# First mixers of a two-block transformer: products by c as ACT copies, forgetting heads without a query bias, division by the softmax sums at the end

## The chip, the core and the metric

The kernel runs on one core of one Trainium2 chip. The metric is the device time of one execution in microseconds (us). The engines of the core are TensorE (PE in the profile; PEld is its weight load), VectorE (DVE), ScalarE (ACT), GpSimd (POOL) and SyncE (SP, which issues most DMAs). They run side by side, each through its own list of instructions in order, and wait for each other by semaphores.

## What is computed

Two blocks over 512 tokens of width 1024, all in 32-bit floats. The first has a modulation from a vector c, four kinds of attention ("mixers") of four heads each, and a feed-forward part; the second has pooling, neighbourhood attention and sixteen experts. What the change touches:

```python
mod = c_act @ ada_w[l] + ada_b[l]          # c_act = silu(c); 1024 -> 6 x 1024
sh_a, sc_a, gt_a, sh_m, sc_m, gt_m = [m[:, None, :] for m in jnp.split(mod, 6, axis=-1)]
...
def forgetting_attention(q, k, v, f_logit, g_q, g_k):
    q = rmsnorm(q, g_q)
    k = rmsnorm(k, g_k)
    log_f = jax.nn.log_sigmoid(f_logit.astype(jnp.float32)).transpose(0, 2, 1)
    cum = jnp.cumsum(log_f, axis=-1)
    def block(i):                           # 128 queries
        s = jnp.einsum('bhqd,bhkd->bhqk', qb, k) * scale
        s = s + (cq[..., :, None] - cum[..., None, :])
        s = jnp.where(dist >= 0, s, NEG)
        p = jax.nn.softmax(s, axis=-1)
        return jnp.einsum('bhqk,bhkd->bhqd', p, v)
...
def neighbourhood_attention(q, k, v, q_norm, k_norm, rpb):   # second block
    s = jnp.einsum('bhcd,bhicjd->bhcij', q_r, k_nb) + bias
    pr = jax.nn.softmax(s.reshape(B, H, GRID_W, kh * WIN_COLS), axis=-1)
    return jnp.einsum('bhcij,bhicjd->bhcd', pr, v_nb)
```

## The kernel before

The program has four stretches. Up to about 60 us the input is normed. From there to about 460 us run the first block's mixers: eight units of two heads each, in the order s0, d0, n0, d1, n1, f0, f1, s1 (s is stick-breaking, d differential, n sparse, f forgetting attention). `run` keeps two units active, advances them step by step in turn, and feeds in between the projections that later units need (`diff_pre`, `fox_pre` and so on), then the output projection. From 460 to about 840 us comes the feed-forward part, to about 1016 us the second block's attention and pooling, and from there the experts, whose weights stream from memory. The order of instructions on each engine isn't written out: a scheduler places each instruction when its inputs are expected, by priority, so that any edit moves rows on every engine.

All mixers share one softmax: `softmax_part` (L610 to L618) adds a bias to the scores on DVE, takes the row's extreme, and lets ACT take the exponential and sum it into `l`. `scale_parts` (L636 to L642) then divides: a reciprocal, and one DVE multiply over each of the two heads' parts `e`. `transpose_p` turns `e` on PE (L626), DVE or ACT copy the result out as `pts`, and `pv` multiplies by the values (L648) into the tile `od`.

`fox` (L850 to L870) goes over four blocks of 128 queries with 128 to 512 keys. For each block and head it makes a bias tile `fb` on DVE: `ckb`, the running sum of the keys broadcast over the partitions, less the query's own `cqc` (L860), plus the causal mask over the last 128 columns (L861). `na` (L1183 to L1207) does four blocks for each of four pairs of heads in the second block.

`ada_more` (L347 to L366) forms four of the six modulation vectors on the side: 64 pieces of 128x512 weights, `adw`, in two buffers. Each piece is loaded by SP, multiplied on POOL by its column of c (L354), and added on POOL into `ada_a`, which has one buffer (L359; the first of eight pieces is copied instead, L357). After eight pieces PE sums over partitions (`pm`, L363). 48 pieces are strewn among the mixers' steps (`ada_side`, every third step), the rest among the first steps of the feed-forward part.

`rstd_rows` takes the sums of squares of a tile's rows and calls `rstd_of` (four small DVE and two small ACT instructions) on eight columns at a time. `to_features` spreads such a row statistic over a tile: one DVE copy `bc` (L392) and four PE transposes `rb` (L396).

## Time and profile before

| | us |
|---|---|
| median of 3 runs | 2147.28 (2143.96 to 2150.56) |
| the profiled execution | 2141.56 |
| its span, first to last instruction | 2139.8 |
| PE busy | 1930.0 |
| DVE busy | 851.3 |
| ACT busy | 555.9 |
| POOL busy | 242.7 |

The profiled execution is 5.7 us under the median, inside what single runs differ by (6.6 us between lowest and highest). All stretches below are given in us from the start of its span. Busy PE time is modelled, since matmuls overlap; the share of an engine is an average over stretches with different limits, so each stretch is read by itself.

### The profile page before, as it was taken

To read this page: it belongs to the slowest core of one execution; us is meant where nothing else is said; L and a number is where in the kernel's file an instruction comes from. 1 tells how busy PE (TensorE), PEld (TensorE's weight loads), DVE (VectorE), ACT (ScalarE), POOL (GpSimd) and SP (SyncE) were. 2 spreads that over 40 slices of the span, in tenths; PEclk is the share of its full clock that TensorE was granted. 3 is DMA by queue.
4 is the path that set the end of the run, shared out by engine and by line. 5 is a ranking of instruction groups with operands and counts; after the bars stand their busy time and mean duration, and the time that the engine had idled before them with its cause. 6 is when DMAs were issued, how large, how long until landed. Compare 5 with 4: busy or idle time off the path is not lost.

```text
span 2139.8 us, 22275 instructions
## 1 busy us (share of the span) xinstructions
PE 1930.0 (90%) x8534; PEld 1067.6 (50%) x8534; DVE 851.3 (40%) x1761; ACT 555.9 (26%) x1089; POOL 242.7 (11%) x211
## 2 busy tenths in 40 slices
PE   3898988979999998999899897878789999999997
PEld 2566666658888887776533232222233333333333
DVE  7887887874444335767431101210010111111114
ACT  4655545533333334444211001100000010000112
POOL 5530433350300000000000000000020000000001
PEclk9998999989999999999899899999989999999998
DMA  6532223243322222222889999799999999999992
GB/s 244 165 121 63 96 61 126 71 117 106 118 99 96 92 98 85 79 84 96 341 363 421 420 422 398 291 420 419 421 410 398 384 375 369 357 365 356 356 391 98
DMA packets 95082, 523.64 MB, mean 245 GB/s; under 512 B 11405, under 2 KB 12853, under 8 KB 44032
## 3 DMA queue, kind: packets, MB, share of 16 engines
q1 hardware_dynamic: 89936, 501.53, 60.6%
q0 software_dynamic: 3552, 17.82, 2.3%
q10 hardware_dynamic: 1488, 2.87, 0.4%
q8 instruction: 67, 1.10, 0.2%
q14 instruction: 39, 0.32, 0.0%
HBM read 510.83 MB, written 4.27 MB: 241 GB/s over the span
## 4 chain that ended last, share of the span: by engine, by line
PE 72%; DVE 11%; DMA 11%; ACT 3%; issue 3%; POOL 1%; POOLq 0%; ACTq 0%; DVEq 0%; SPq 0%
PE ua L1659 5%; PE ga L1659 5%; PE ga L1660 4%; DMA ch<-in_w_de_dram 4%; PE yd L1690 4%; PE ua L1660 4%; PE yd L1689 3%; PE pg L1594 3%; DMA ch<-in_w_ue_dram 3%; PE z L1609 3%; DMA xg<-xd,at 2%; PE od L648 2%; PE ag L331 2%; PE ag L332 2%; PE ag L333 2%
## 5 line engine op out<-in xcount | busy, mean ns | idle before, releaser
L1659 PE MATMUL ga<-ch,xe 128*64 128x512 f32 x512 | 244.4, 613 | 1.8 <-DMA ch<-in_w_ge_dram 1.8
L1660 PE MATMUL ua<-ch,xe 128*64 128x512 f32 x512 | 237.1, 611 | 5.9 <-DMA ch<-in_w_ue_dram 5.9
L1690 PE MATMUL yd<-ch,hts 128*64 128x512 f32 (+1 forms) x544 | 231.1, 572 | 10.4 <-DMA ch<-in_w_de_dram 10.4
L1659 PE MATMUL ua<-ch,xe 128*64 128x512 f32 x512 | 239.8, 612 | 0.1
L1660 PE MATMUL ga<-ch,xe 128*64 128x512 f32 x512 | 239.0, 610 | 0.5 <-DMA ch<-in_w_ge_dram 0.5
L1689 PE MATMUL yd<-ch,hts 128*64 128x512 f32 (+1 forms) x544 | 232.8, 572 | 0.0
L324 DVE TENSOR_TENSOR wlo<-pan,whi 128x1024 fp32r<-128x1024 f32 x119 | 154.6, 1299 | 157.0 <-ACT whi L321 153.9
L321 ACT ACTIVATE whi<-pan 128x1024 fp32r<-128x1024 f32 x119 | 125.9, 1058 | 211.7 <-PE ag L332 93.5
L1668 DVE TENSOR_TENSOR sg<-sg,ua 128x512 f32<-128x512 f32 x32 | 22.0, 687 | 340.2 <-PE ua L1660 340.2
L1690 PEld LDWEIGHTS yd<-ch,hts 128*64 128x64 f32 x544 | 70.1, 136 | 99.5 <-issue 76.5
L337 DVE TENSOR_TENSOR ys<-yg,ys 128x512 fp32r<-128x512 f32 (+1 forms) x17 | 12.5, 733 | 256.9 <-ACT ys L336 256.9
L1660 PEld LDWEIGHTS ua<-ch,xe 128*64 128x64 f32 x512 | 68.3, 140 | 83.0 <-issue 71.5
L1659 PEld LDWEIGHTS ua<-ch,xe 128*64 128x64 f32 x512 | 67.5, 140 | 80.7 <-issue 79.5
L1660 PEld LDWEIGHTS ga<-ch,xe 128*64 128x64 f32 x512 | 66.2, 139 | 74.4 <-issue 70.4
L1659 PEld LDWEIGHTS ga<-ch,xe 128*64 128x64 f32 x512 | 65.6, 139 | 70.8 <-issue 67.3
L1689 PEld LDWEIGHTS yd<-ch,hts 128*64 128x64 f32 x544 | 69.3, 136 | 56.4 <-issue 55.2
L1672 ACT ACTIVATE hts<-pth 128x512 f32<-128x512 f32 x32 | 19.1, 595 | 270.7 <-PE pth L1671 270.7
L1693 ACT ACTIVATE yg<-yd,gs 128x512 f32<-128x512 f32 (+1 forms) x17 | 11.3, 662 | 286.9 <-PE yd L1690 158.5
L354 POOL TENSOR_TENSOR adw<-adw,cT 128x512 f32<-128x512 f32 x64 | 77.4, 1210 | 41.3 <-DMA adw<-in_ada_dram 40.9
L359 POOL TENSOR_TENSOR ada_a<-ada_a,adw 128x512 f32<-128x512 f32 x56 | 78.0, 1393 | 4.4
L617 ACT ACTIVATE e<-e,m 128x256 f32<-128x256 f32 (+8 forms) x128 | 65.0, 509 | 51.2 <-DVE m L615 47.4
L1476 POOL DMA_INDIRECT xg<-xd,at x7 | 6.9, 979 | 594.8 <-DVE at L1474 590.4
(895 smaller groups left out, 3834.4 us busy)
## 6 DMA issues: line engine op xcount, KB each, us to landing
ch<-in_w_de_dram SPq DMA_DIRECT2D x128, 1024.0 KB, 13.6
ch<-in_w_ue_dram SPq DMA_DIRECT2D x125, 1024.0 KB, 8.9
ch<-in_w_ge_dram SPq DMA_DIRECT2D x120, 1024.0 KB, 12.4
pan<-in_w_up_dram SPq DMA_DIRECT2D x44, 512.0 KB, 3.2
adw<-in_ada_dram SPq DMA_DIRECT2D x64, 256.0 KB, 2.7
pan<-in_w_in_dram SPq DMA_DIRECT2D x24, 512.0 KB, 4.0
pan<-in_w_dn_dram SPq DMA_DIRECT2D x22, 512.0 KB, 3.3
adr<-in_adaT_dram SPq DMA_DIRECT2D x8, 1024.0 KB, 9.2
```

The lines of the kernel that those rows point to most:

```text
L321: A.activation(hi, raw, AF.Copy)
L324: eng.tensor_tensor(lo, raw, hi.bitcast(FT), op=OP.subtract)
L331: T.matmul(out, wh, xh, start=first, stop=False)
L354: P.tensor_tensor(w, w, cT[:, k:k + 1].to_broadcast([128, 512]), op=OP.mult)
L359: P.tensor_tensor(ada_next[1], ada_next[1], w, op=OP.add)
L617: A.activation(e[:, :nk], e[:, :nk], AF.Exp, bias=m, scale=-1.0, accum_out=l)
L1594: T.matmul(pg, xf[:, k], ple["wg"][k // 2][:, k % 2, S * h:S * h + S], start=k == 0, stop=k == 7)
L1609: T.matmul(zl[h], yts[at[k][0]][:, at[k][1]], ple["wg"][k // 2][:, k % 2, S * h:S * h + S], start=k == 0, stop=k == 7)
L1659: T.matmul(acc_[m][0:64], xe[:, kk, 0:64], wa[:, k], start=kk == 0, stop=kk == 7)
L1660: mm = T.matmul(acc_[m][64:128], xe[:, kk, 64:128], wb[:, k], start=kk == 0, stop=kk == 7)
L1689: T.matmul(yd[0:64], hts[:, kk, 0:64], wa[:, k_], start=kk == 0, stop=kk == 15)
L1690: mm = T.matmul(yd[64:128], hts[:, kk, 64:128], wb[:, k_], start=kk == 0, stop=kk == 15)
```

## The change

Four edits:

- In `ada_more` the product by a column of c is now the scale of an ACT copy. The first of eight pieces goes by it straight into `ada_a`, the others into `adw` in place; POOL only adds.
- In `fox` the query's own running sum is no longer subtracted: it is the same over a row, and the softmax doesn't see it. The causal mask is added in place to `ckb`, once for both heads, and the blocks run from the last to the first so that a masked stretch isn't read again. `cqc` and the copies that made it are gone.
- In `fox` and `na` the parts aren't divided any more. The sums of all four blocks stay in one tile, and the new function `divided` divides the output of a pair of heads once: a copy from PSUM, a reciprocal, `to_features`, one multiply. In `na` it goes through another tile, from which the two reordering copies read.
- `rstd_rows` calls `rstd_of` once for up to 16 columns; its two small tiles have 16 columns and four buffers.

```diff
-            P.tensor_tensor(w, w, cT[:, k:k + 1].to_broadcast([128, 512]), op=OP.mult)
             if k == 0:
                 ada_next[1] = tmp[0].tile([128, 512], FT, name="ada_a", tag="ada_a", bufs=1)
-                P.tensor_copy(ada_next[1], w)
+                A.activation(ada_next[1], w, AF.Copy, scale=cT[:, 0:1])
             else:
+                A.activation(w, w, AF.Copy, scale=cT[:, k:k + 1])
                 P.tensor_tensor(ada_next[1], ada_next[1], w, op=OP.add)
...
-        v, y = sm([128, 8], "rv")[0:n, 0:out.shape[-1]], sm([128, 8], "ry")[0:n, 0:out.shape[-1]]
+        v, y = [sm([128, 16], n_, 4)[0:n, 0:out.shape[-1]] for n_ in ("rv", "ry")]
...
-        for c in range(0, 4 * n, 8):
-            rstd_of(ms[:, c:min(c + 8, 4 * n)], scale, y[:, c:min(c + 8, 4 * n)])
+        rstd_of(ms[:, 0:4 * n], scale, y)
...
+    def divided(o, l, out):
+
+        A.activation(out, o, AF.Copy)
+        r = sm([128, 8], "r8", 2)
+        V.reciprocal(r, l)
+        V.tensor_tensor(out, out, to_features(r, 2), op=OP.mult)
...
     def fox(hp):
         q, kk, v, ckb = st["fox", hp]
         o = ps("od", "o", 2)
-        for i in range(4):
+        ls_ = sm([128, 4, 2], "l8", 2)
+
+
+        for i in (3, 2, 1, 0):
             nk = 128 * (i + 1)
-            l = sm([128, 2], "l2")
             e = []
+            V.tensor_tensor(ckb[:, :, nk - 128:nk], ckb[:, :, nk - 128:nk], K["cm"].unsqueeze(1).to_broadcast([128, 2, 128]),
+                            op=OP.add)
             for par in range(2):
-                h = 2 * hp + par
-                fb = t2k("fb")
-                V.tensor_scalar(fb[:, :nk], ckb[:, par, :nk], cqc[:, 4 * i + h:4 * i + h + 1], None, op0=OP.subtract)
-                V.tensor_tensor(fb[:, nk - 128:nk], fb[:, nk - 128:nk], K["cm"], op=OP.add)
                 s = ps("s", "s", 2)
                 scores(s, q, kk, par, slice(128 * i, 128 * i + 128), 0, nk)
-                e.append(softmax_part(s, fb[:, :nk], nk, l[:, par:par + 1]))
+                e.append(softmax_part(s, ckb[:, par, :nk], nk, ls_[:, i, par:par + 1]))
             yield
-            scale_parts(e, l, nk)
...
-        A.activation(mix[:, 2 + hp], o, AF.Copy)
+        divided(o, ls_.rearrange("p i h -> p (i h)"), mix[:, 2 + hp])
...
     def na(hp):
...
-            scale_parts(e, l, nk)
...
-        m, o = mix2[:, 4 + hp].rearrange("p (r c) -> p c r", r=8), o.rearrange("p (c r) -> p c r", r=8)
+        t = p2k("on")
+        divided(o, l.rearrange("p i h -> p (i h)"), t)
+        m, o = mix2[:, 4 + hp].rearrange("p (r c) -> p c r", r=8), t.rearrange("p (c r) -> p c r", r=8)
```

What the scheduler makes of it, first on DVE in forgetting attention. In the kernel before, around a block of 256 keys: `fb` is the bias tile, `e` a softmax part, `s` the scores, `m` the row's extreme, and the other rows belong to the sparse unit and to projections.

```order
L860 TENSOR_SCALAR fb<-ckb,cqc 128x256
L567 SCALAR_TENSOR_TENSOR sq<-pr,gsc,rb 128x512
L861 TENSOR_TENSOR fb<-fb,cst 128x128
L638 RECIPROCAL r_2922<-l_2882 128x2
L560 COPY pr<-acc__2989 128x512
L615 ISA e,m<-s,fb 128x256
```

And in the changed kernel, in the second forgetting unit from its second block on:

```order
L862 TENSOR_TENSOR ckb<-ckb,cst 128x2x128
L632 COPY pts<-pt 128x512
L614 ISA e,m<-s,ckb 128x384
L614 ISA m 128x1
L614 ISA e,m<-s,ckb 128x384
L614 ISA m 128x1
L862 TENSOR_TENSOR ckb<-ckb,cst 128x2x128
```

Of a block there remain on DVE one mask, two reductions with their small second row, and a copy of the transposed part; no row stands between the exponential on ACT and the transpose on PE.

Next on ACT, where the sparse unit's compressed keys begin (`kcv`). In the kernel before:

```order
L784 ACTIVATE kcv<-acc__954 64x512 x2
L321 ACTIVATE whi<-pan 128x1024
L617 ACTIVATE e,l_917<-e,m 128x128 x2
L574 ACTIVATE q_831<-sq 64x512 x2
L631 ACTIVATE pts<-pt 128x128
L617 ACTIVATE e,l_983<-e,m 128x256 x2
L321 ACTIVATE whi<-pan 128x1024
L617 ACTIVATE e,l_1011<-e,m 128x256 x2
```

And in the changed kernel:

```order
L787 ACTIVATE kcv<-acc__936 64x512 x2
L356 ACTIVATE ada_a<-adw,cT 128x512
L630 ACTIVATE pts<-pt 128x128
L616 ACTIVATE e,l_965<-e,m 128x256 x2
L358 ACTIVATE adw<-adw,cT 128x512 x2
L616 ACTIVATE e,l_993<-e,m 128x256 x2
L358 ACTIVATE adw<-adw,cT 128x512
L630 ACTIVATE pts<-pt 128x256
```

The products stand singly or in twos between the exponentials of the active units; each waits for its piece's DMA, and the one into `ada_a` for the `pm` of the eight pieces before it.

That `pm` stands on PE of the changed kernel just behind the projection that `kcv` is copied from:

```order
L654 MATMUL od<-pts,va 64x128
L703 MATMUL s<-k_724,k_480 128x256 x2
L333 MATMUL acc__936<-hTh,wlo 128x512
L363 MATMUL pm<-cst,ada_a 128x1 x4
L331 MATMUL acc__1223<-hTh,whi 128x512
```

In the kernel before POOL alone stood behind such a `pm`; now it is ACT, and behind ACT's product the exponentials.

On POOL a product and an addition stood in turn before; now additions alone stand there, 42 of them in one row.

## Rows read from the trace of the kernel before

**Rows 1.** The page: busy time by engine, and the chain by engine

```profile
PE 1930.0 (90%) x8534; PEld 1067.6 (50%) x8534; DVE 851.3 (40%) x1761; ACT 555.9 (26%) x1089; POOL 242.7 (11%) x211
...
PE 72%; DVE 11%; DMA 11%; ACT 3%; issue 3%; POOL 1%; POOLq 0%; ACTq 0%; DVEq 0%; SPq 0%
```

**Rows 2.** Stretches: length, busy PE, PEld, DVE, ACT, POOL, clock, DMA share, GB/s

```profile
60.00:460.00 400.00, 352.11 (x1874) 254.19 (x1872) 321.63 (x804) 202.67 (x489) 144.13 (x116) 0.94 0.32 99
460.00:840.00 380.00, 371.54 (x1631) 305.48 (x1630) 174.76 (x215) 131.81 (x161) 25.85 (x24) 0.99 0.30 101
840.00:1016.00 176.00, 171.76 (x875) 130.80 (x876) 120.83 (x318) 78.19 (x182) 6.82 (x13) 0.97 0.26 83
```

**Rows 3.** The chain: shares by line, 60 to 460; pieces as start, us, what

```profile
by line: PE od L648 6.8%; PE pt L626 5.8%; DVE e L642 3.8%; issue 3.6%; DVE wlo L324 3.2%; PE ms L382 3.0%; PE od L919 2.4%; PE s L816 2.4%; DVE e L615 2.2%; DVE e L705 1.8%; DVE q L575 1.6%; DVE sq L409 1.3%; DVE x L1013 1.3%; PE tl L914 1
...
277.88 2.37 DVE e L642 x2
```

**Rows 4.** Timeline (start, us) of DVE and of POOL at 66 us

```profile
66.65 3.36 DVE L324 TENSOR_TENSOR wlo<-pan,whi 128x1024 fp32r<-128x1024 f32 x1 [0.65 <-ACT whi L321]
...
66.87 2.04 POOL L354 TENSOR_TENSOR adw<-adw,cT 128x512 f32<-128x512 f32 x2
```

**Rows 5.** DVE groups, 60 to 460: count, busy us, mean ns, idle before

```profile
L324 DVE TENSOR_TENSOR wlo<-pan,whi 128x1024 fp32r<-128x1024 f32 x31 | 43.9, 1415 | 3.7 <-ACT whi L321 2.6 <-ACT ckb L846 0.7 <-PE acc__1241 L333 0.3
L642 DVE TENSOR_SCALAR e<-e,r 128x384 f32<-128x384 f32 x12 | 11.0, 954 | 0.1
L409 DVE TENSOR_TENSOR sq<-sq 128x512 f32<-128x512 f32 x7 | 10.4, 1480 | 2.2 <-ACT sq L407 2.2
L861 DVE TENSOR_TENSOR fb<-fb,cst 128x128 f32<-128x128 f32 x16 | 8.5, 532 | 0.3
L640 DVE TENSOR_TENSOR r<-r,gates 128x2 f32<-128x2 f32 x24 | 7.0, 291 | 0.4
L642 DVE TENSOR_SCALAR e<-e,r 128x128 f32<-128x128 f32 x12 | 6.5, 568 | 0.1
```

**Rows 6.** The same operations where POOL rests: 840 to 1016, and 480 to 840

```profile
L324 DVE TENSOR_TENSOR wlo<-pan,whi 128x1024 fp32r<-128x1024 f32 x20 | 24.4, 1221 | 0.4 <-ACT whi L321 0.2
L642 DVE TENSOR_SCALAR e<-e,r 128x248 f32<-128x248 f32 x24 | 7.3, 345 | 0.2
...
L409 DVE TENSOR_TENSOR sq<-sq 128x512 f32<-128x512 f32 x6 | 4.1, 684 | 0.0
```

**Rows 7.** POOL's two groups, 100 to 480

```profile
L359 POOL TENSOR_TENSOR ada_a<-ada_a,adw 128x512 f32<-128x512 f32 x42 | 58.5, 1392 | 3.3
L354 POOL TENSOR_TENSOR adw<-adw,cT 128x512 f32<-128x512 f32 x48 | 57.8, 1205 | 31.3 <-DMA adw<-in_ada_dram 31.0
```

**Rows 8.** Busy DVE time of lines L642, L860, L638, 60 to 460

```profile
60.00:460.00 400.00, 33.48 (x64) 0.94 0.32 99
...
60.00:460.00 400.00, 8.17 (x16) 0.94 0.32 99
...
60.00:460.00 400.00, 5.14 (x32) 0.94 0.32 99
```

**Rows 9.** Nearest rows to what is added: 60 to 460, 840 to 1016, page

```profile
L392 DVE COPY bc<-rs 128x512 f32<-128x512 f32 x13 | 6.6, 507 | 0.2
L567 DVE SCALAR_TENSOR_TENSOR sq<-pr,gsc,rb 128x512 f32<-128x512 f32 x6 | 4.5, 743 | 0.5 <-PE rb L396 0.5
...
L396 PE MATMUL rb<-cst,bc 128*128 128x128 f32 x32 | 5.8, 274 | 0.0
...
L1693 ACT ACTIVATE yg<-yd,gs 128x512 f32<-128x512 f32 (+1 forms) x17 | 11.3, 662 | 286.9 <-PE yd L1690 158.5
```

**Rows 10.** Waits, 100 to 480: us in total, times, longest

```profile
POOL ada_a L357 <- PE pm L363: 180.7, 5, 61.6
...
POOL adw L354 <- DMA adw<-in_ada_dram: 31.0, 24, 5.8
```

**Rows 11.** PE's weight loads of the transposes, 840 to 1016

```profile
L626 PEld LDWEIGHTS pt<-cst,e 128*128 128x128 f32 x40 | 5.5, 140 | 4.9 <-DVE e L642 2.1 <-DVE pts L633 0.6 <-DVE sq L567 0.6
```

More of the change, by code (lines that the diff above doesn't have):

```diff
@@ L722, in _build @@
     cum = pa.tile([4, S], FT, name="cum")
-    cqc = pa.tile([128, 16], FT, name="cqc")
     def gates_and_decay():
@@ L739, in gates_and_decay @@
         V.tensor_tensor_scan(cum, f2[0:4], f[0:4], 0.0, op0=OP.mult, op1=OP.add)
-        V.tensor_copy(t[0:4], cum)
         pg = ps("pg", "pt", 2)
@@ L746, in gates_and_decay @@
         V.tensor_scalar(gates[:, 0, 0:4], gates[:, 0, 0:4], K["vcol"], None, op0=OP.mult)
-        V.tensor_copy(cqc.rearrange("p (t c) -> p t c", t=4), pg[:, :, 0:4])
     def compress(kv):
@@ L1185, in na @@
         o = ps("od", "o", 2)
+        l = sm([128, 4, 2], "l8", 2)
         for b in range(4):
             nk = 248 if b else 256
-            l = sm([128, 2], "l2")
             e = []
@@ L1197, in na @@
                     T.matmul(s[:, :nk], q[:, par, 128 * b:128 * b + 128], k_, start=x_ == 0, stop=x_ == 1)
-                e.append(softmax_part(s, nb[:, par, 0:248] if b else nb[:, par, 248:], nk, l[:, par:par + 1]))
+                e.append(softmax_part(s, nb[:, par, 0:248] if b else nb[:, par, 248:], nk, l[:, b, par:par + 1]))
             yield
-            scale_parts(e, l, nk)
             pts = [transpose_p(e[par], nk, par) for par in range(2)]
```

## The prediction

> **What bounds the kernel now.** I read the page first, for the share of each engine in the chain that ended last [rows 1], and then the busy time by stretches, because such a share is a mean over stretches with different limits. In the stretch of the first block's mixers, 60 to 460 us, DVE is busy 321.6 of 400 us and PE 352.1; in the feed-forward stretch PE is busy 371.5 of 380, in the second block's attention 171.8 of 176 [rows 2]. The last two go by PE, and work taken off DVE there buys nothing by itself. The mixers go by nothing alone: there the chain changes between PE, DVE and a little ACT, and its largest DVE lines are the division of the softmax parts (L642, 3.8%) and the low parts of the weights (L324, 3.2%) [rows 3]. The third view is the same operation in and out of that stretch. `wlo` takes 1415 ns among the mixers and 1221 where POOL rests, the sum of squares L409 takes 1480 against 684 [rows 5, 6]. The timeline shows why: a `wlo` that starts at 66.65 lasts 3.36 us, and two products by c run on POOL from 66.87 for 2.04 us meanwhile [rows 4]. A DVE operation that meets a POOL operation stands until that one is over. So the mixers pay for POOL's work, though POOL itself is 1% of the chain [rows 1].
>
> **What the change does, part by part.** All sums are made against the profiled execution, 2141.56 us (a span of 2139.8 and 1.8 around it), and moved to the median of the runs, 2147.28, at the end; two executions differ by about 0.3% without a cause, and that is also what a measurement of this kernel can tell from no change.
>
> *Products by c leave POOL.* Five DVE groups tell what POOL costs DVE among the mixers. L324: 31 x (1415 - 1221) = 6.0 us. L642 on 384 columns: the row without POOL has 345 ns for 248 columns, so at most 534 for 384, and 12 x (954 - 534) = 5.0. L642 on 128 columns, at most 345: 12 x (568 - 345) = 2.7. L409: 7 x (1480 - 684) = 5.6. L640 against a reciprocal of the same two columns, 5.14 / 32 = 0.161: 24 x (291 - 161) = 3.1. Together 22.4 us [rows 5, 6, 8]. Groups that I leave out could double it. POOL's products have 57.8 us of the 116.3 that products and additions take [rows 7]; the additions stay. So half goes, 11.1 us. I count all of it on the path, because the stretched instructions are the ones that others wait for: a pair of L642, on 128 columns, stands in the chain with 2.37 us where two undisturbed ones would take at most 0.69 [rows 3, 6].
>
> *Forgetting heads.* The subtraction L860 goes: 8.2 us in 16 instructions [rows 8]. Of the masks L861, 8.5 us in 16 [rows 5], eight remain, twice as wide; they cost between half and all of that, and I take 3.0 saved. L642 has 64 instructions with 33.5 us among the mixers [rows 8], and 16 of them are the forgetting heads': 8.4. Eight reciprocals of 0.161 make 1.3. Sum 20.9 us.
>
> *Row statistics.* The four norms of the differential heads need one `rstd_of` each instead of two: 16 small DVE instructions of about 0.16, 2.6 us.
>
> *What comes back on DVE.* Two divisions of an output: a reciprocal 0.161, the copy `bc` 0.507, a multiply with one input in PSUM, whose nearest row is L567 with 0.743 [rows 9]. That is 1.4 each, 2.8 us.
>
> So beside the 11.1 us there are 20.9 + 2.6 - 2.8 = 20.7 us of DVE work less, 31.8 in all. How much of those 20.7 lies on the path? L642 has 3.8% of 400 us, 15.2, in the chain and 33.5 of busy time; L324 12.8 of 43.9; L409 5.2 of 10.4 [rows 3, 5, 8]. That is 33.2 of 87.8, some 0.4. I count 8.3 us, and DVE's part of the sum is 11.1 + 8.3 = 19.4.
>
> What one reads into these rows hangs on which engine is the limit. In the mixers DVE is busy 80% of the time and PE's weight loads 64% (254.2 of 400) [rows 2]. The Trainium skill, Perfetto Trace Analysis, section Identifying the Most-Contended Engine, says to judge DVE by its occupancy, PE by its weight loads rather than by its matmuls' busy time, and to count the engine that comes out highest as the one to relieve. By that rule DVE is the limit and the whole 31.8 us would come off, not 19.4. The chain disagrees so far: PE has 72% of it and DVE 11% over the kernel [rows 1].
>
> *Products on ACT.* An ACT copy with a column as scale: the nearest row is L1693, a Copy with such a scale, 662 ns [rows 9]. 48 of them among the mixers are 31.8 us, in a stretch where ACT is busy 202.7 of 400 [rows 2]. ACT has 3% of the span in the chain, 64 us of its 555.9 busy [rows 1]: 11.5%. So 3.7 us on the path; none if they fall into ACT's idle half, 31.8 if each delays an exponential that others wait for. The 16 in the feed-forward part lie under PE, which is busy there 98% of the time; without that cover they would cost 10.6.
>
> *New waits on ACT.* Each product waits for its piece's DMA. POOL stood 31.0 us for these, 24 times, because nothing else was queued there [rows 10]. On ACT the exponentials stand behind it. In ACT's order the products stand among other work, so that much of the landing has passed; I take half of the 31.0 and ACT's 11.5% of it, 1.8 us, between 0 and 31.0. The products that go into `ada_a` also wait for the `pm` of eight pieces before. POOL stood 180.7 us for that in 5 waits, up to 61.6 [rows 10]. On PE this `pm` stands directly behind the projection for which the ACT row ahead of the product waits too, so I put nothing for it; a place where PE is behind its order is part of the rival on ACT. SP's queue is involved as well: the next load of `adw` waits there for POOL's addition, and the weight panels are queued behind it. That was so before, with POOL's two operations in the loop instead of one of ACT and one of POOL.
>
> *PE.* Four transposes for each division, 0.274 us each [rows 9]: eight are 2.2 us among the mixers, of which PE's share of the chain, 72%, is 1.6.
>
> *The second block's attention.* 32 instructions of L642 and 16 reciprocals go, but PE is busy there 98%. What PE gets back is what it stood for them: 2.1 us at the weight loads of the transposes [rows 11]. It gets 16 transposes more, 4.4 us. Net 2.3 us slower. The last unit's output takes a copy and a multiply more before the reordering copies, some 1.4 us; the output projection's first half lies over it, and if that cover is short it costs up to this.
>
> Sum: -19.4 + 3.7 + 1.8 + 1.6 + 2.3 = -10.0 us. From 2141.56 that gives 2131.6, and from the median 2147.28 some **2137 us**. The prologue and the expert stretch have no edit and move as a whole with the start of their work.
>
> **Rivals.** *DVE is the limit of the mixers.* All 31.8 us come off and ACT's additions fall into its idle half: -31.8 + 1.6 + 2.3 = -27.9, so 2119; with the groups left out it could be 2108. For it speak DVE's 80% and the stretched pieces in the chain; against it PE's 88% of modelled busy time. This is what the skill's rule above amounts to.
>
> *PE is the limit of the mixers.* Then DVE's relief goes into waits that nobody notices, and PE's 2.2 and the second block's 2.3 remain: +4.5, 2152, no change that can be told. For it speaks PE's share of the chain; against it that PE's lines in the chain are short pieces, transposes and products with the values, that start when DVE or ACT is done.
>
> *The additions hit instead.* POOL still runs the additions, 42 of 1.39 us [rows 7]. If a DVE operation that no longer meets a product meets an addition, the 11.1 us stay: -10.0 + 11.1 = +1.1, 2148. Against it speaks that POOL's busy time halves; for it, that the pieces then follow each other faster.
>
> *ACT becomes the one that others wait for.* Its products and their waits are 31.8 + 31.0 = 62.8 us. If half of that lies on the path, 31.4, the sum is -19.4 + 31.4 + 1.6 + 2.3 = +15.9, and the time 2163. It turns slower at all from 25% on the path ((19.4 - 3.9) / 62.8) and slower by over 0.3%, 6.4 us, from 35%. ACT's present 11.5% speaks against it; for it, that an engine works its list in order and that each softmax goes through ACT, so that one late `adw` holds up both active units. The place is the rows with two products in a row between exponentials.
>
> **How the numbers follow.** The forecast has a chance of 0.46, DVE as the limit 0.24, PE as the limit 0.11, the additions 0.09, ACT 0.10. The forecast by itself reaches from 2130 to 2144: DVE's share of 0.4 may be 0.2 or 0.6 (4 us each way), ACT's may be double or nothing (5.5). Some 0.35 of its 0.46 lie below 2140.8, where faster by over 0.3% begins, and 0.11 above. So faster is 0.35 + 0.24 = 0.59, the same 0.11 + 0.11 + 0.09 = 0.31, slower 0.10. The range reaches on the fast side to the rival of DVE with a part of the groups left out, 2110, and on the slow side over PE as the limit to 2156, with some of a mild case of ACT; it leaves out the bad case of ACT and a gain beyond all of DVE's relief.
>
> **What would show it.** In the changed kernel's profile, the stretch from 60 us to the end of the mixers should be some 12 us shorter, its DVE time about 32 us less and its ACT time about 32 more. `wlo` among the mixers should come half way from 1415 to 1221 ns; if it stays, the additions hit instead. ACT's waits on the DMA of `adw` and on `pm` should sum to under 16 us; much over that, with exponentials late behind them, shows the rival on ACT. The second block's stretch should be 2 to 3 us longer. The forecast is wrong if the mixers' stretch shrinks by DVE's whole relief, or if it doesn't while DVE's time does.

## The result, and the profile after

The changed kernel takes 2115.55 us, the median of 4 runs (2114.46 to 2117.49). The kernel before, on the same chip, takes 2148.92 (2143.96 to 2152.56). The ratio is 0.985, with an interval of 0.983 to 0.987: 1.5% or 33 us faster. The forecast was 10 us; the direction was right, the time lies in the range, and the gain is three times the one worked out. The profiled execution took 2117.49 us, 24 less than the one before; the latter was one of the shorter runs of its kernel. The executions of the kernel before differ with the mean granted clock of TensorE: twelve of them on one chip, taken beside the runs below, go from 2138.59 us at 0.966 of full speed to 2153.93 at 0.957. The four of the changed kernel lie between 0.963 and 0.966, and the two profiled executions have 0.965 and 0.966. So some 24 us is the difference at a like clock, and the other 9 may go with the clock; whether the change raises it isn't shown.

The page of the changed kernel: its span, the busy time by engine with its share and count, and the chain by engine, to be read against [rows 1].

```profile
span 2115.7 us, 22322 instructions
...
PE 1927.1 (91%) x8558; PEld 1070.2 (51%) x8558; DVE 803.3 (38%) x1665; ACT 595.6 (28%) x1149; POOL 156.7 (7%) x139
...
PE 71%; DMA 11%; DVE 6%; ACT 3%; issue 2%; POOL 0%; POOLq 0%; ACTq 0%; DVEq 0%; SPq 0%
```

DVE lost 48 us of busy time and POOL 86, ACT gained 40; in the chain DVE's share fell from 11% to 6%. The page says what moved between engines, not where the gain is. For that I cut both spans at the same places of the work: the first matmul of the feed-forward part, the pause on PE ahead of the second block's first norm, the router's first matmul, and the end. In each row: the stretch and its length, then busy PE, PEld, DVE, ACT and POOL, the granted clock, DMA's share and GB/s. First the kernel before (the mixers ran up to 466.6 us; [rows 2] were cut at 460):

```profile
60.00:466.60 406.60, 354.10 (x1882) 255.72 (x1880) 324.84 (x811) 204.48 (x494) 147.36 (x118) 0.94 0.32 99
466.60:840.00 373.40, 369.55 (x1622) 303.94 (x1622) 171.55 (x209) 130.00 (x157) 22.62 (x21) 0.99 0.30 100
840.00:1015.80 175.80, 171.56 (x875) 130.68 (x875) 120.83 (x318) 78.19 (x182) 6.62 (x13) 0.97 0.26 82
1015.80:2139.80 1124.00, 1013.62 (x4096) 363.23 (x4095) 187.91 (x369) 115.32 (x215) 34.34 (x40) 0.96 0.91 370
```

and the kernel after:

```profile
60.00:438.40 378.40, 351.01 (x1889) 257.15 (x1887) 282.06 (x751) 237.81 (x543) 70.86 (x53) 0.95 0.34 107
438.40:811.60 373.20, 369.86 (x1622) 304.12 (x1622) 170.34 (x208) 134.10 (x163) 13.08 (x14) 0.99 0.30 100
811.60:988.00 176.40, 171.71 (x890) 132.05 (x890) 116.75 (x283) 80.57 (x186) 6.36 (x12) 0.97 0.25 79
988.00:2115.70 1127.70, 1013.40 (x4096) 362.99 (x4095) 188.03 (x370) 115.32 (x215) 34.59 (x40) 0.96 0.91 369
```

The mixers are 28.2 us shorter, the feed-forward part and the second block's attention keep their length (-0.2 and +0.6), and the expert stretch is 3.7 longer. That last one has no edit, and the same work took between 1120 and 1128 us in the executions of the versions below; it is scatter. So in this pair the whole gain lies in the mixers. PE does the same work there (354.10 against 351.01) in less time. DVE is 42.8 us less busy, ACT 33.3 more, POOL 76.5 less.

DVE's 42.8 can be divided by the duration of single instructions. These are DVE's groups among the mixers of the kernel after (60 to 438.4 us: count, busy us, mean ns, idle before), to be read against [rows 5] and [rows 6]:

```profile
L324 DVE TENSOR_TENSOR wlo<-pan,whi 128x1024 fp32r<-128x1024 f32 x31 | 39.5, 1275 | 6.5 <-ACT whi L321 5.8 <-PE acc__936 L333 0.3
...
L408 DVE TENSOR_TENSOR sq<-sq 128x512 f32<-128x512 f32 x7 | 7.6, 1088 | 2.1 <-ACT sq L406 2.1
...
L639 DVE TENSOR_TENSOR r<-r,gates 128x2 f32<-128x2 f32 x24 | 5.7, 239 | 0.4
...
L641 DVE TENSOR_SCALAR e<-e,r 128x384 f32<-128x384 f32 x8 | 4.1, 541 | 0.0
L862 DVE TENSOR_TENSOR ckb<-ckb,cst 128x256 f32<-128x256 f32 x8 | 3.4, 421 | 0.1
...
L641 DVE TENSOR_SCALAR e<-e,r 128x128 f32<-128x128 f32 x8 | 2.0, 284 | 0.1
```

`wlo` came from 1415 to 1275 ns, where 1221 is undisturbed: 72% of the way, not half. The sum of squares (L409 before, L408 now) came from 1480 to 1088, half of the way to 684. The divisions of 384 columns fell from 954 to 541 and those of 128 from 568 to 284; where POOL does none of this work (x_noadd, below) they take 417 and 280, so that is three quarters of the way and nearly all of it.

What is left of the disturbance shows at single instructions. Two places of the timeline of the kernel after, DVE and POOL (start, us, and in brackets the idle time before):

```profile
250.46 0.16 DVE L707 RECIPROCAL r<-l 128x2 f32<-128x2 f32 x1
250.58 0.17 DVE L375 TENSOR_TENSOR rv<-rv,ry 128x8 f32<-128x8 f32 x1
250.66 1.25 DVE L709 TENSOR_TENSOR c<-r,ls 128x1 f32<-128x1 f32 x1
...
250.58 1.32 POOL L359 TENSOR_TENSOR ada_a<-ada_a,adw 128x512 f32<-128x512 f32 x1 [18.34 <-ACT ada_a L356]
```

```profile
420.67 1.78 DVE L408 TENSOR_TENSOR sq<-sq 128x512 f32<-128x512 f32 x1
...
420.45 1.44 POOL L359 TENSOR_TENSOR ada_a<-ada_a,adw 128x512 f32<-128x512 f32 x1 [0.79 <-ACT adw L358]
```

A product of one column, 128x1, takes 1.25 us: it starts at 250.66 and ends at 251.91, and POOL's addition ends at 251.90. The sum of squares starts at 420.67, the addition ends at 421.89, and the sum of squares ends at 422.45, 0.56 later; undisturbed it takes 0.68 in all. In both places DVE stands for nearly all of the time until POOL is done. Nothing of that appears as a wait; it is counted as busy time of DVE.

So I summed it over the mixers for every kernel below: for each DVE instruction the time above the lower quartile of its line and shape in the same whole trace, where that is over 60 ns. I call the sum the **stretch**. It is worked out from the rows of single instructions, not a row itself. POOL's count leaves out three DMA issues.

```
mixers of one execution  length   DVE busy  stretch (instr.)  ACT busy  POOL busy (instr.)
before                   406.6    325       56.4 (76)         205       147 (115)
after                    378.4    282       21.1 (29)         238        71 (50)
p_ada                    382.8    287       18.7 (23)         238        71 (50)
p_bias                   401.8    318       55.9 (72)         206       150 (115)
p_divfox                 413.1    322       53.9 (76)         206       151 (115)
p_rstd                   406.8    321       51.5 (71)         204       155 (115)
u_ada                    397.1    306       46.7 (70)         203       152 (115)
u_na                     380.0    282       20.6 (30)         238        71 (50)
u_rstd                   376.8    273       14.4 (19)         238        73 (50)
x_act2                   388.4    279       19.2 (25)         265        71 (50)
x_noadd                  367.4    260        0.0 (0)          241         3 (1)
x_lock                   391.0    292       33.4 (68)         238       130 (148)
x_memset                 383.7    276       17.9 (32)         237       122 (246)
f_dve                    377.9    288        0.0 (0)          208         3 (1)
```

Where POOL does none of this work (x_noadd, f_dve) the sum is 0, so it holds little else than standing for POOL. Before, 56.4 of DVE's 325 us were standing: 23.7 of it beside products and the copies that begin a group, 32.6 beside additions (each instruction is put to the one of POOL that it overlaps longest). After, 21.1 is left. Of the 42.8 us that DVE lost, then, 35.3 is stretch and only 7.5 is work. The length of a single execution varies by some us (p_divfox's mixers are longer than before's, its median time isn't), so the experiments are judged by their medians and the table by its large steps.

### The profile page after: what moved, and what is told of

It is laid out like the page before. It is cut to its first block, busy times and chain, and to the rows that moved or that the text cites. A ratio compares the mean times of both kernels' runs of the same rounds, so it can differ in the third digit from the quotient of the medians.

```text
span 2115.7 us, 22322 instructions
## 1 busy us (share of the span) xinstructions
PE 1927.1 (91%) x8558; PEld 1070.2 (51%) x8558; DVE 803.3 (38%) x1665; ACT 595.6 (28%) x1149; POOL 156.7 (7%) x139
## 4 chain that ended last, share of the span: by engine, by line
PE 71%; DMA 11%; DVE 6%; ACT 3%; issue 2%; POOL 0%; POOLq 0%; ACTq 0%; DVEq 0%; SPq 0%
PE ua L1662 6%; PE ga L1662 5%; PE ga L1663 4%; DMA ch<-in_w_de_dram 4%; PE yd L1693 4%; PE ua L1663 4%; PE yd L1692 3%; DMA ch<-in_w_ue_dram 3%; PE pg L1597 3%; PE z L1612 3%; DMA xg<-xd,at 3%; PE od L654 2%; PE ag L331 2%; PE ag L332 2%; PE ag L333 2%
## 5 line engine op out<-in xcount | busy, mean ns | idle before, releaser
L324 DVE TENSOR_TENSOR wlo<-pan,whi 128x1024 fp32r<-128x1024 f32 x119 | 149.6, 1257 | 163.0 <-ACT whi L321 160.4
L331 PE MATMUL ag<-hTh,whi 128*128 128x512 f32 x176 | 70.8, 403 | 2.2 <-ACT hTh L428 2.2
L1670 ACT ACTIVATE sg<-ga 128x512 f32<-128x512 f32 x32 | 19.0, 595 | 185.5 <-PE ga L1663 172.9
```

What stands on the lines that cost most here:

```text
L324: eng.tensor_tensor(lo, raw, hi.bitcast(FT), op=OP.subtract)
L331: T.matmul(out, wh, xh, start=first, stop=False)
```

## The experiments

Two theories stood for the 33 us. **A, the lock:** the products left POOL, DVE stands less for POOL, and the standing lay on the path. **B, the softmax path:** the forgetting heads lost a subtraction, half of their masks and the divisions, which shortens the chain from scores to probabilities. A third reading, that the loop of the loads turns faster with one POOL instruction less in it, shares A's edit and had to be told from it. Each run stands beside runs of the kernel before on the same chip, and ratios are to these. "Over" or "under the kernel after" is a difference of medians from different rounds. The medians of the kernel before in these rounds lie between 2147.08 and 2149.64, so such a difference is good to about 3 us.

### Each part alone, on the kernel before

**p_ada**: only the products, as scales of ACT copies.

```
-            P.tensor_tensor(w, w, cT[:, k:k + 1].to_broadcast([128, 512]), op=OP.mult)
             if k == 0:
-                P.tensor_copy(ada_next[1], w)
+                A.activation(ada_next[1], w, AF.Copy, scale=cT[:, 0:1])
             else:
+                A.activation(w, w, AF.Copy, scale=cT[:, k:k + 1])
                 P.tensor_tensor(ada_next[1], ada_next[1], w, op=OP.add)
```

> The kernel before with the products by c as scales of ACT copies and nothing else. Theory A (the lock: the time that DVE stands for POOL falls by far more than half, and all of it lies on the path): 15 to 25 us faster than before, with DVE's busy time among the mixers some 30 us less. Theory B (the gain comes from the shorter softmax of the forgetting heads): 3 to 8 us faster, as the prediction's own sum for this part, -11.1 + 3.7 + 1.8 = -5.6.

Measured: 2118.97 us against 2147.64, ratio 0.987 (0.984 to 0.991), 28.7 us faster. The rows of its mixers, the stretch first and then two DVE groups:

```profile
60.00:442.80 382.80, 347.81 (x1877) 257.58 (x1875) 286.46 (x810) 237.30 (x551) 71.47 (x53) 0.94 0.34 105
...
L324 DVE TENSOR_TENSOR wlo<-pan,whi 128x1024 fp32r<-128x1024 f32 x31 | 39.2, 1264 | 5.0 <-ACT whi L321 3.6 <-PE pt L626 0.7 <-ACT ckb L846 0.5
...
L409 DVE TENSOR_TENSOR sq<-sq 128x512 f32<-128x512 f32 x7 | 8.5, 1221 | 2.1 <-ACT sq L407 2.1
```

DVE executes 810 instructions as before (811), and is busy 38.4 us less: all of it is duration. This one edit brings most of the gain, more than A's 15 to 25 us and far more than B's 3 to 8. A stands as the main cause.

**p_bias**: only the forgetting heads without a query bias, the masks put on the key bias in place, the blocks in reversed order.

```
-        for i in range(4):
+        for i in (3, 2, 1, 0):
...
+            V.tensor_tensor(ckb[:, :, nk - 128:nk], ckb[:, :, nk - 128:nk], K["cm"].unsqueeze(1).to_broadcast([128, 2, 128]),
+                            op=OP.add)
...
-                fb = t2k("fb")
-                V.tensor_scalar(fb[:, :nk], ckb[:, par, :nk], cqc[:, 4 * i + h:4 * i + h + 1], None, op0=OP.subtract)
-                V.tensor_tensor(fb[:, nk - 128:nk], fb[:, nk - 128:nk], K["cm"], op=OP.add)
...
-                e.append(softmax_part(s, fb[:, :nk], nk, l[:, par:par + 1]))
+                e.append(softmax_part(s, ckb[:, par, :nk], nk, l[:, par:par + 1]))
```

> The kernel before with the forgetting heads' query bias left out, the mask added once in place and the blocks from last to first, and nothing else. By the prediction's sum 11.2 us of DVE work less, 0.4 of it on the path: 4 us faster. Theory A: 3 to 6. Theory B: 8 to 14 us faster.

Measured: 2138.24 us, ratio 0.996 (0.994 to 0.998), 9.4 us faster. DVE is 7.6 us less busy, and the stretch stays (55.9). That gain lies in B's range and above A's.

**p_divfox**: only the division of the forgetting heads' output at the end.

```
+    def divided(o, l, out):
+
+        A.activation(out, o, AF.Copy)
+        r = sm([128, 8], "r8", 2)
+        V.reciprocal(r, l)
+        V.tensor_tensor(out, out, to_features(r, 2), op=OP.mult)
...
-            scale_parts(e, l, nk)
...
-        A.activation(mix[:, 2 + hp], o, AF.Copy)
+        divided(o, ls_.rearrange("p i h -> p (i h)"), mix[:, 2 + hp])
```

> The kernel before with the division at the end in the forgetting heads only. By the prediction's sum 9.7 us of DVE work less, 2.8 back, 0.4 of that on the path, and 1.6 us more on PE: 1 us faster. Theory A: 0 to 3 us faster. Theory B (no DVE row between the exponential and the transposes): 6 to 12 us faster.

Measured: 2145.4 us, ratio 0.999 (0.997 to 1.001), no change that can be told. DVE is 3 us less busy. B expected 14 to 26 us of these two edits; they bring 11.6 together, most of it by the first. As the main cause B falls; as a smaller one it keeps those 9.4 us.

**p_rstd**: only the row statistics of four norms in one call on up to 16 columns, not two on 8.

```
-        v, y = sm([128, 8], "rv")[0:n, 0:out.shape[-1]], sm([128, 8], "ry")[0:n, 0:out.shape[-1]]
+        v, y = [sm([128, 16], n_, 4)[0:n, 0:out.shape[-1]] for n_ in ("rv", "ry")]
...
-        for c in range(0, 4 * n, 8):
-            rstd_of(ms[:, c:min(c + 8, 4 * n)], scale, y[:, c:min(c + 8, 4 * n)])
+        rstd_of(ms[:, 0:4 * n], scale, y)
```

> The kernel before with one call for up to 16 columns of row statistics, and nothing else. Both theories: within 2 us of the kernel before; 2.6 us of small DVE work goes.

Measured: 2152.07 us, ratio 1.003 (1.001 to 1.005), 4.4 us slower, just outside of no change. Fewer DVE instructions don't pay here.

The four medians add up to -28.7 - 9.4 - 2.2 + 4.4 = -35.9 us, and all parts together gave -33.4. Nothing large is missing.

### Parts taken back out of the kernel after

**u_ada**: the products go back to POOL (p_ada's diff reversed).

> The changed kernel with the products by c back on POOL. Theory A: loses 15 to 25 us of the 33 and ends 8 to 18 us faster than the kernel before. Theory B: loses 3 to 8 and stays 25 to 30 us faster than the kernel before.

Measured: 2136.19 us, ratio 0.996 (0.994 to 0.998), 20.6 us over the kernel after. Its mixers, and `wlo`:

```profile
60.00:457.10 397.10, 351.60 (x1886) 258.28 (x1884) 306.14 (x750) 202.38 (x486) 152.06 (x118) 0.94 0.33 102
...
L324 DVE TENSOR_TENSOR wlo<-pan,whi 128x1024 fp32r<-128x1024 f32 x31 | 44.3, 1430 | 1.5 <-ACT whi L321 1.3
```

With about the same number of DVE instructions (750 and 751) the stretch is back from 21.1 to 46.7 and `wlo` at 1430. That is A from the other side, inside its 15 to 25 us.

**u_na**: the neighbourhood heads' division back in each block.

```
-        l = sm([128, 4, 2], "l8", 2)
         for b in range(4):
+            l = sm([128, 2], "l2")
...
+            scale_parts(e, l, nk)
...
-        t = p2k("on")
-        divided(o, l.rearrange("p i h -> p (i h)"), t)
-        m, o = mix2[:, 4 + hp].rearrange("p (r c) -> p c r", r=8), t.rearrange("p (c r) -> p c r", r=8)
+        m, o = mix2[:, 4 + hp].rearrange("p (r c) -> p c r", r=8), o.rearrange("p (c r) -> p c r", r=8)
```

> The changed kernel with the neighbourhood attention's division back at each block. The prediction put that edit at 2.3 us slower, so this would be 2 us faster than the changed kernel; the trace of the changed kernel shows the second block's stretch as long as before, so 0 to 1 us of difference either way is expected, some 33 us under the kernel before.

Measured: 2115.2 us, ratio 0.985 (0.982 to 0.989), the same as the kernel after. In the second block the division costs and saves nothing that can be told.

**u_rstd**: the row statistics back in two calls (p_rstd's diff reversed).

> The changed kernel with row statistics in two calls of eight columns again. Alone that edit made the kernel before 0.3% slower, with nothing in its own work that could (it only takes instructions away). If that is the order of the whole list: within 4 us of the changed kernel, either way. If one call of 16 columns is itself worse (the first eight columns wait for the others): 4 to 8 us faster than the changed kernel.

Measured: 2111.92 us (2110.47 to 2114.56), ratio 0.984 (0.981 to 0.986). The interval overlaps that of the kernel after, but both directions of this edit, 4.4 and 3.6 us, say that the single call is no gain. This run also has less stretch than the kernel after (14.4 against 21.1), so its 3.6 us need not come from the call itself. Of the versions that compute the whole result it is the fastest measured.

### The suspected costs by themselves

**x_act2**: on the kernel after, a second ACT copy of each piece.

```
             k = m % 8
+            A.activation(w, w, AF.Copy)
             if k == 0:
```

> The changed kernel with a second ACT copy of each modulation piece ahead of the first: 48 copies more among the mixers, some 32 us of ACT. If ACT's added time lies on the path by its 11.5% of the chain: 4 us slower than the changed kernel. If each delays an exponential that others wait for: up to 32 us slower. If ACT's idle time takes it all: no difference.

Measured: 2120.8 us, ratio 0.986 (0.982 to 0.990), 5 us over the kernel after, with overlapping intervals. Its mixers, and ACT's waits for the loads (total, times, longest):

```profile
60.00:448.40 388.40, 358.47 (x1889) 264.56 (x1887) 279.02 (x751) 264.78 (x599) 71.42 (x53) 0.91 0.33 104
...
ACT adw L354 <- DMA adw<-in_ada_dram: 6.5, 9, 1.7
```

27 us more of ACT cost at most about 5 of time. They need not be ACT's: with the same 1889 matmuls PE is 7.5 us busier here than in the kernel after, at a granted clock of 0.91 against 0.95. The copies are cheap, as they would be if ACT's idle time took most of them; whether they are free isn't shown.

**x_noadd**: on the kernel after, no additions; each sum of eight pieces is replaced by its last piece, so the modulation is computed from an eighth of its terms.

```
                 A.activation(w, w, AF.Copy, scale=cT[:, k:k + 1])
-                P.tensor_tensor(ada_next[1], ada_next[1], w, op=OP.add)
             if k == 7:
+                ada_next[1] = w
```

> The changed kernel without POOL's additions (each sum is formed from its last piece alone, so the modulation is not the reference's); loads and ACT copies stay. It measures what POOL still costs. The changed kernel's trace shows DVE operations among the mixers some 20 us longer than where POOL rests. Theory A: 12 to 20 us faster than the changed kernel. If the additions' lock lies beside the path: 0 to 5 us.

Measured: 2101.1 us, ratio 0.978 (0.974 to 0.981), 14.5 us under the kernel after. Its mixers, and two DVE groups:

```profile
60.00:427.40 367.40, 351.20 (x1889) 261.66 (x1887) 259.13 (x751) 239.99 (x545) 3.36 (x4) 0.94 0.35 111
...
L324 DVE TENSOR_TENSOR wlo<-pan,whi 128x1024 fp32r<-128x1024 f32 x31 | 37.9, 1221 | 3.7 <-ACT whi L321 3.0
...
L408 DVE TENSOR_TENSOR sq<-sq 128x512 f32<-128x512 f32 x7 | 4.8, 689 | 2.3 <-ACT sq L406 2.1
```

With POOL silent both groups run at their undisturbed 1221 and 689 ns, and no instruction is stretched any more. What the additions still cost the kernel after is at most these 14.5 us.

**x_lock**: on the kernel after, two POOL products of 128x192 on a tile of their own behind each addition. They read and write, and nothing uses what they make; the next addition stands behind them on POOL, in this run and in the next alike.

```
-                P.tensor_tensor(ada_next[1], ada_next[1], w, op=OP.add)
+                done_ = P.tensor_tensor(ada_next[1], ada_next[1], w, op=OP.add)
+                with tc.issue_after(done_.ins):
+                    for _ in range(2):
+                        P.tensor_tensor(lk, lk, one.to_broadcast([128, 192]), op=OP.mult)
```

> The changed kernel with two more POOL multiplies of 128x192 behind each addition, in a tile of their own: POOL reads and writes on-chip memory about as long as with the products, but no load and no ACT copy waits for them. If what counted in the products was that DVE stands while POOL reads: 12 to 24 us slower than the changed kernel, and DVE operations among the mixers longer by 45 us or more in sum, as in the kernel before (56) against 21 in the changed one. If it was the loop of loads behind POOL on SP's queue: within 4 us of the changed kernel.

Measured: 2127.85 us (2125.55 to 2132.21) against 2147.08, ratio 0.992 (0.989 to 0.995), 12.3 us over the kernel after. POOL's new group and DVE's `wlo` among its mixers:

```profile
L364 POOL TENSOR_TENSOR lk<-lk,one 128x192 f32<-128x192 f32 x98 | 61.3, 626 | 3.8
...
L324 DVE TENSOR_TENSOR wlo<-pan,whi 128x1024 fp32r<-128x1024 f32 x31 | 41.3, 1331 | 6.4 <-ACT whi L321 5.6 <-PE acc__944 L333 0.3
```

**x_memset**: the same with four POOL memsets of that tile, which write and don't read.

```
+                    for _ in range(4):
+                        P.memset(lk, 1.0)
```

> The same with four memsets of 128x192 in place of the two multiplies: POOL is as busy, but only writes. In the trace before, a DVE operation beside a memset of 1.80 us kept its 0.69 us. If POOL's reads are what DVE stands for: within 4 us of the changed kernel. If any POOL work does it: as slow as with the multiplies.

Measured, on the same chip: 2117.27 us (2114.82 to 2119.71), ratio 0.987 (0.984 to 0.990), 1.7 us over the kernel after and not to be told from it. The same two groups:

```profile
L364 POOL MEMSET lk<- 128x192 f32 x196 | 52.4, 267 | 8.5
...
L324 DVE TENSOR_TENSOR wlo<-pan,whi 128x1024 fp32r<-128x1024 f32 x31 | 39.3, 1268 | 4.7 <-ACT whi L321 4.2
```

POOL was made 59 us busier by the one and 51 by the other. The reading products lengthened DVE's stretch by 12.3 us (21.1 to 33.4) and the kernel by 12.3; the memsets did neither that can be told (17.9, and 1.7 us). Between these two runs, which share a chip and nearly a clock in the mixers (0.92 and 0.93), lie 15.5 us of stretch and 10.6 us of time. So it is POOL's reads that cost, and not its time or its place in the loop of the loads. I had expected the stretch of x_lock to come back to 45 or more. It didn't: the new products last 626 ns, half of the old ones' 1205, and beside them a DVE instruction is stretched by 0.29 us in the mean, where it was 0.65 beside the old ones. The Trainium skill, SBUF — State Buffer, section Who interferes with whom, says that DVE and GpSimd share a port pair, which is an exclusive lock, and that a DVE instruction with two inputs in SBUF contends with a GpSimd instruction that reads SBUF, not with one that only writes. Both runs agree with it: of DVE's `TENSOR_TENSOR` instructions that ran beside the new POOL instructions and no others of POOL's, 22 of 33 were stretched in x_lock and none of 31 in x_memset. The memsets aren't wholly without effect: eight copies and products by a column lasted 61 to 152 ns longer beside them, 0.85 us in all.

**f_dve**: on the kernel after, product and addition as one DVE instruction; POOL does none of it, and ACT keeps only the first piece of each eight.

```
-                A.activation(w, w, AF.Copy, scale=cT[:, k:k + 1])
-                P.tensor_tensor(ada_next[1], ada_next[1], w, op=OP.add)
+                V.scalar_tensor_tensor(ada_next[1], w, cT[:, k:k + 1], ada_next[1], op0=OP.mult, op1=OP.add)
```

> The changed kernel with product and addition in one DVE instruction (weights times the column of c, plus the sum so far), 42 among the mixers at about 0.75 us, so 32 us of DVE more; POOL does nothing there and ACT's 42 copies go. DVE operations stand for nobody, 21 us less. If DVE's busy time decides: 32 - 21 = 11 us more of it, 5 to 9 us slower than the changed kernel. If ACT's copies and their waits cost more than 5 us: no difference or faster.

Measured: 2115.17 us, ratio 0.985 (0.982 to 0.988), the same as the kernel after. Its mixers, and two DVE groups:

```profile
60.00:437.90 377.90, 351.78 (x1892) 262.12 (x1890) 288.00 (x799) 208.32 (x493) 3.36 (x4) 0.94 0.34 107
...
L324 DVE TENSOR_TENSOR wlo<-pan,whi 128x1024 fp32r<-128x1024 f32 x31 | 37.8, 1220 | 3.5 <-ACT whi L321 3.4
L358 DVE SCALAR_TENSOR_TENSOR ada_a<-adw,cT,ada_a 128x512 f32<-128x512 f32 x49 | 36.6, 746 | 2.1 <-DMA adw<-in_ada_dram 1.1 <-ACT ada_a L356 0.9
```

DVE does product and addition of 49 pieces for 36.6 us and saves the 21.1 of stretch, and ACT saves 30. The 5 to 9 us that DVE's busy time was to cost didn't come. POOL's help with the additions is worth nothing in the kernel after. With the products on POOL too its help costs: u_ada is 21 us slower than this run.

## Why the prediction came out too small

**The step that failed is the term "Products by c leave POOL".** It was put at 11.1 us off, and with ACT's 3.7 and 1.8 the products' move was to bring 5.6. Alone it brought 28.7 (p_ada), with 37.7 us of stretch gone where the term has 11.1 (56.4 to 18.7), and 20.6 came back with it (u_ada). The mechanism was the right one; the size was made of two factors, the first far too small and the second somewhat.

- *The whole.* I took five groups' 22.4 us for all of what POOL cost DVE. The stretch over all groups was 56.4. I wrote that the groups left out could double it, gave that to a rival's lower end, and left the sum as it was. By the same summing over the trace of before, L642 alone had 13.8 over all its shapes, where I counted 7.7; left out were the differential heads' division L705 (3.9), L861 (3.9), `k` L582 (3.5), `kp` L906 (3.0) and others with less.
- *The half that stays.* I halved it by POOL's time. 35.3 of 56.4 went, 63%, and 67% in p_ada; between u_ada and the kernel after it is 55%. The additions alone stretch DVE by 21.1 after, where it was 32.6 beside additions before. In u_ada, with the products back, it is 21.1 beside additions too, so the products ahead of them don't explain it; why the additions hit less than before isn't shown by a run.

The third factor, "all of it on the path", was a little high. u_ada: 25.6 us more stretch for 20.6 us of time, and up to 25.6 if the 5 us of x_act2 are ACT's and are given back. x_lock: 12.3 for 12.3 against the kernel after, 15.5 for 10.6 against x_memset. x_noadd: 21.1 for 14.5. A microsecond of standing costs 0.7 to 1 us here.

The sentence that a DVE operation that meets a POOL operation stands until that one is over was too wide. Beside POOL's products, additions and copies in the trace of before, 45 of 68 `TENSOR_TENSOR` and 20 of 34 `TENSOR_SCALAR` instructions of DVE were stretched, but only 8 of 31 `SCALAR_TENSOR_TENSOR`, and none of the 32 reductions of the softmax (L615) and the 17 reciprocals.

**Forgetting heads and divisions: two errors that partly cancel.** For p_bias and p_divfox I counted 20.9 - 2.8 = 18.1 us of DVE work less, 0.4 of it on the path, and 1.6 of PE against it: 5.6 us. The busy time that p_bias and p_divfox took off is 7.6 + 3.0, because the old durations held stretch that I had counted already in the first term, and because neighbouring small DVE instructions overlap in the trace (in the rows above L375 ends at 250.75 and L709 has begun at 250.66). Yet the two gained 11.6 us: about all of what they took off counts. The 0.4 out of the chain's shares was too low and the work too high, and the two errors left half of the gain.

**Row statistics: wrong sign.** 2.6 us less work was expected; alone the edit costs 4.4, just clear of the noise, and 3.6 in the changed kernel, which isn't clear of it. One call has to wait for all of its columns' sums, where the first of two calls could start early; this is argued, no run shows it.

**ACT: right in size, as far as it is shown.** A copy took 716 ns where 662 was taken, 57 of them in all (50 in the row below). ACT's waits were 14.7 us for the loads and 3.9 for `pm`, for which the sum had nothing: 18.6 together, a little over the 16 that I had put as the sign. Here are those rows of the kernel after, ACT's group and its waits (total, times, longest):

```profile
L358 ACT ACTIVATE adw<-adw,cT 128x512 f32<-128x512 f32 x50 | 35.3, 716 | 15.0 <-DMA adw<-in_ada_dram 14.7
...
ACT adw L358 <- DMA adw<-in_ada_dram: 14.7, 16, 2.5
ACT ada_a L356 <- PE pm L363: 3.9, 2, 2.9
```

By x_act2 such a load costs at most about 5 us of time, against 5.5 in the sum. The rival on ACT is refuted.

**PE and the second block: small.** PE stayed at 351 us among the mixers (354 before). The second block was to be 2.3 us longer and is 0.6 longer, within scatter; u_na says the same, so that term isn't seen.

**The rivals.** "The additions hit instead" is refuted by the stretch, 56.4 to 21.1, and by `wlo` at 1275. "PE is the limit" is refuted by the mixers' 28 us at an unchanged PE. "DVE is the limit", 2119 with a lower end of 2108, came nearest. That the time lies in the range is owed to this rival, for whose sake the range reached so far, and not to the forecast. By its own condition DVE's whole relief comes off: DVE lost 42.8 us, the mixers 28.2 in the profiled pair and the kernel 33 by the medians, two thirds to three quarters, with 33 us more on ACT to pay for. The prediction drew this rival from the Trainium skill, Perfetto Trace Analysis, section Identifying the Most-Contended Engine, and by these numbers the trace backs that rule in part. It doesn't back it wholly: f_dve has DVE 5.9 us busier than the kernel after at the same time. And DVE's 80% held 56.4 us in which it did no work. The question "which engine is the limit" had hidden the other one, of what an engine's busy time is made.

In the chain of the kernel after (shares by line, 60 to 438.4) that can be seen once more, against [rows 3]:

```profile
by line: PE od L654 8.1%; PE pt L625 5.5%; PE ms L382 2.9%; PE s L819 2.7%; issue 2.4%; ACT whi L321 2.2%; DVE wlo L324 1.9%; PE rb L395 1.7%; DMA adw<-in_ada_dram 1.5%; PE ck L848 1.5%; DVE e L641 1.4%; PE s L596 1.3%; PE od L921 1.1%; PE 
```

DVE's division (L642 before, L641 now) fell from 3.8% to 1.4%, `wlo` from 3.2% to 1.9%, and no DVE line stands among the first six. The chain now goes mainly over PE.

## What to carry to other kernels

Where POOL runs elementwise work beside a busy DVE, first sum up how much longer DVE's instructions last than the same shapes do where POOL rests, over all groups and not the largest ones; DVE's busy time minus that sum is its work. Standing of that kind is in no list of waits, and it was worth 0.7 to 1 of its length here, so work on POOL that reads SBUF may cost the path more than the same work on ACT, or fused on DVE itself. And where the executions of one kernel differ with the granted clock, two kernels are best compared at a like clock too. When a sum leaves something out that "could double" a term, the sum must carry it, not the edge of the range.

## What the runs showed of the hardware

The prediction took any POOL operation for one that DVE stands for. It depends almost wholly on POOL's reads: 196 memsets of 52.4 us left `wlo` at 1268 ns, 98 products of 61.3 us brought it to 1331, with 1275 without either. I had not expected that it strikes the smallest instruction with the whole rest of POOL's: a 128x1 product took 1.25 us, where its neighbours of 128x2 and 128x8 took 0.16 and 0.17, as do most others of its own line. And the whole of product and addition fused on DVE took 746 ns a piece, barely more than ACT's copy alone (716), and about half of POOL's addition alone (1378):

```profile
L359 POOL TENSOR_TENSOR ada_a<-ada_a,adw 128x512 f32<-128x512 f32 x49 | 67.5, 1378 | 285.0 <-ACT ada_a L356 188.6 <-ACT adw L358 86.7 <-ACT ry L373 8.7
```

What stays open is how much of x_noadd's 14.5 us is stretch and how much the shorter loop of loads (the stretch that went, 21.1 us, would be enough for all of it), and whether 9 of the 33 us go with the granted clock and the change itself raises it.
